# Attention's row maxima: split on VectorE and turned as float16 products a step later; value sums begun by their own products

## The chip, the cores and the metric

The kernel runs on one core of one Trainium2 chip. The metric is device time of one execution in microseconds (us). The core has five engines that each work through a queue of their own in order: TensorE (PE in the profile; PEld is its weight load), VectorE (DVE), ScalarE (ACT), GpSimd (POOL) and SyncE (SP), which issues the DMAs. An instruction waits for semaphores that other engines raise; whatever stands behind it in the same queue waits with it.

## What is computed

One layer over 2048 tokens of width 1024 with a context of 256 tokens: a modulation, a bidirectional retention of 4 heads, grouped attention (8 query heads, 2 key heads, head size 64), an output product, and a feed-forward part of width 4096. The change touches the attention alone:

```python
def _dense_attention(q, k, v):
    s = jnp.einsum('bqkgd,bskd->bkgqs', q, k).astype(jnp.float32) * ATT_SCALE
    p = jax.nn.softmax(s, axis=-1).astype(v.dtype)
    return jnp.einsum('bkgqs,bskd->bqkgd', p, v)
```

Keys and values are those of context and tokens together, 2304 rows, which are 18 tiles of 128.

## The kernel before

The work on 128 tokens is a tile; a `Group` is one tile with one key head and its four query heads. There are 32 groups, `order` counts the tiles from the last to the first and gives each tile an even group (`g` = 0) and an odd one. The program is written out step by step: `on(k, phase, ...)` puts a call into step `k`, and every step runs its calls phase by phase in the order of `PHASES` (scores, piece, maximum, early, exp, cast, low, chain, pe, values, late, dma). A group takes 18 steps for its maxima and, from 22 steps after its first, 18 for its scores, so that in one step TensorE works on the scores of one group and on the maxima of the next. Two groups make a block of 36 steps, into which `retention` and `output_tile` lay their own products (`bank` tiles) and what belongs to them on the other engines.

Per group:

- `piece` and `maximum` (L169 to L187): 18 products of queries and keys into PSUM tiles `mp`, of which there are two, and from each VectorE's negative maxima into `nm`, five for each head and 128 queries.
- `least` (L189 to L193): two reductions of `nm` into columns 64 and 96 of `mt`, a float32 tile with one 128 column part for each head; column 80 holds a constant from the start (L1431).
- `turn` (L195 to L198), a step later: four float32 transposes of `mt` into an `mp` tile, so that the maxima lie along the free axis in rows 64, 80 and 96.
- `rows` (L201): ScalarE writes rows 64 to 127, divided by `ROW` = 8192, as float16 into the second half of the queries `qr`. `rows2` (L205), a step after that: VectorE writes the rest of the division into rows 96 to 127, from the same PSUM tile.
- `scores` (L211, L212): two products into `st`, the second with keys that hold 8192 in rows 64, 80 and 96 (`unit`), which subtracts the maximum. `exp` (L217) makes `p` on ScalarE, two tiles of it are cast to float16 `phi` (`cast`, L221), and the rest becomes `plo` on GpSimd for pairs 0, 2, 4, 6 and 7 (L228) and on VectorE for the others, one half in each of two steps (L230).
- `values` (L232 to L245): products of `plo` (65 columns) and `phi` (129 columns) with the values into the sums `o`. The sums of a group begin with two products of a tile of zeros, 258 columns each (L236).

What stands around it and is named below: `norm` (L1600), two at a time on ScalarE, and the gate product (L1604, `oo<-oo,ogate`) on GpSimd, both of the retention; `add` (L1730, `xr`) on VectorE and `square` (L1737, into `oat`) on ScalarE, of the output tile; L1817 on GpSimd, of `h_pair`, in four of the later blocks; L1670 on VectorE and L1687 on SyncE, once at the beginning, of `output_scales`.

Of the kernel before, what the change touches and what calls it, by code (L numbers as in the profile page):

```python
# [11 lines left out]
F32 = mybir.dt.float32  # L12
F32R = mybir.dt.float32r
F16 = mybir.dt.float16
BF16 = mybir.dt.bfloat16
I32 = mybir.dt.int32
AF = mybir.ActivationFunctionType
ALU = mybir.AluOpType
AX = mybir.AxisListType
# [3 lines left out]
P = 128  # L23
# [6 lines left out]
NK = NT + NC  # L30
H = 4
CH = 128
HD = 64
# [3 lines left out]
PSHIFT = 8  # L37

ROW = 8192.0
VW = 2 * HD + 1  # L40
# [16 lines left out]
def layer_kernel(ctx: ExitStack, tc: tile.TileContext, a: dict, out: bass.AP):  # L57
    nc = tc.nc
    mm = nc.tensor.matmul
# [4 lines left out]
    ident = const.tile([P, P], F32, name="ident")  # L64
# [76 lines left out]
    wv = None  # L141
    early = kp.tile([P, NK * (VW + 1)], F32, name="early", tag="wv")
# [6 lines left out]
    class Group:  # L149
# [14 lines left out]
                nc.sync.dma_start(q[64:, 0, :, e], src[:, 0])  # L164

        def minima(self, pool):
            self.nm = pool.tile([P, 2, 2, 5], F32, name="nm", tag="nm")

        def piece(self, i, pool=None, tag="mp"):  # L169
            m = self.m[i] = (pool or psS).tile([P, 512], F32, name="mp", tag=tag)  # L170
# [17 lines left out]

        def least(self, mt):  # L189
            self.mt = mt  # L190
            nm = self.nm.rearrange("p a b c -> p (a b) c")
            for c in (64, 96):
                nc.vector.tensor_reduce(mt[:, :, c], nm, axis=AX.X, op=ALU.min)  # L193

        def turn(self):  # L195
            self.m = psS.tile([P, 4, P], F32, name="mp", tag="mp")
            for h in range(4):
                nc.tensor.transpose(self.m[:, h], self.mt[:, h], ident)  # L198

        def rows(self):  # L200
            nc.scalar.activation(self.qr[64:, 1], self.m[64:], AF.Copy, scale=1 / ROW)  # L201

        def rows2(self):
            lo = self.qr[96:, 1]
            nc.vector.scalar_tensor_tensor(lo, self.m[96:], 1 / ROW, lo, op0=ALU.mult, op1=ALU.subtract)  # L205

        def scores(self, kt):
            ps = self.s[kt] = psS.tile([P, 512], F32, name="st", tag="st")
# [23 lines left out]
        def values(self, j):  # L232
            if j == 0:
                self.o = [psV.tile([P, 2, VW], F32, name=f"o{b}", tag=f"o{b}") for b in range(2)]
                for o in self.o:
                    mm(o, zeros, wv[:, 0, :2, :VW], start=True, stop=False)  # L236
            hi, lo = self.hi.pop(j), self.lo.pop(j)
            for i in range(2):
                v = wv[:, self.g, 2 * j + i]
                for h in range(4):  # L240
                    o = self.o[h // 2][:, h % 2]
                    c = slice(h * P, (h + 1) * P)
                    last = 2 * j + i == NK - 1 and h % 2 == 1
                    mm(o[:, : HD + 1], lo[:, i, c], v[:, : HD + 1], start=False, stop=False)  # L244
                    mm(o, hi[:, i, c], v[:, :VW], start=False, stop=last)  # L245

        def evacuate(self):
            self.so = op.tile([P, 4, VW], F32, name="so", tag="so")
# [20 lines left out]
    with ExitStack() as st, tc.manual_schedule():  # L269
# [5 lines left out]
        op = st.enter_context(tc.tile_pool(name="op", bufs=2, reuse_waits="tile"))  # L275
# [143 lines left out]
        def turn_rows(end):  # L419
            def use(s, x):  # L420
                def turn():
                    x["t"] = columns(x["b"][:64], 4, psO.tile([P, 4, P], F32, name="psc", tag="pso"))

                do(s, "turn", turn)
                do(s + 1, "vec", lambda: end(x["t"]))

            return use
# [251 lines left out]
        def post(s, g, col, kind, i, x):  # L679
# [23 lines left out]
            if col in (C_RQ, C_RK):  # L703
# [27 lines left out]

                late = s + 4 + (s < 5)
                do(late, "turn", turn)
                do(late + 1, "turned", turned)
                do(late + 2, "store", lambda: nc.sync.dma_start(dst.rearrange("p (h t) -> p h t", h=H), x["z"]))
# [17 lines left out]
            elif col == C_AQ:  # L753
# [12 lines left out]
                    lambda: bc(x["r"].unsqueeze(2), [P, 8, HD]),  # L766
                )
                do(s + 4, "turn", turn)

                def high():  # L770
# [158 lines left out]
        def ff_scales(s):  # L929
# [73 lines left out]
            for i, what in enumerate((bounds, rows, results)):  # L1003
                do(s + 5 + i, "aux", what)
# [181 lines left out]
        units, first = [], {}  # L1186
# [10 lines left out]
        for (g, col), w in weights.items():  # L1197
# [4 lines left out]
            for j in range(w.n):  # L1202
                f, h = s - 5 + j, s - 3 + j if j < 2 else s - 1
                if (g, col) == (1, C_RQ):
                    f, h = s - 9 + j, (s - 6, s - 5, s - 2, s - 2)[j]
                f, h = f - early_by, h - early_by
# [13 lines left out]
        for n, tile_of in enumerate(GROUPS[1]):  # L1220
            b = first[0, C_RV] + 3 + n + n // 6
            rows, x = Rows([tile_of], 1), {}

            def turn(n=n, rows=rows, x=x):
                kind, i = GROUPS[1][n]
                hs[1, n] = new_h(1, kind, i)
                x["p"] = [Part(kind, rows.x[0], hs[1, n], k, 4) for k in (0, 4)]
                for p in x["p"]:
                    p.turn()

            def each(what, x=x):
                for p in x["p"]:
                    getattr(p, what)()

            do(b - 4, "load", rows.load, 0)
            do(b - 2, "hi", rows.square, 0)
            do(b - 1, "hi", rows.root)
            do(b, "vec", rows.norm, 0)
            do(b, "turn", turn)
            do(b + 1, "vec", each, "scale")  # L1240
            do(b + 1, "pool", each, "shift")
            do(b + 2, "hi", each, "high")
            do(b + 3, "low", each, "low")
# [161 lines left out]
    def pool(stack, name, bufs=1, **kw):  # L1405
        return stack.enter_context(tc.tile_pool(name=name, bufs=bufs, reuse_waits="tile", **kw))

    qp = pool(attn, "qp", 2)
    op = pool(attn, "op2", 2)
    vp = pool(attn, "vp")  # L1410
# [11 lines left out]
    for g in range(2):  # L1422
        nc.sync.dma_start(ks2[:64, g], ks[:64, g])
        nc.sync.dma_start(ks2[64:, g], a["unit"])
    zeros = vp.tile([P, P], F16, name="zeros")
    nc.vector.memset(zeros, 0.0)
    mts = [vp.tile([P, 4, P], F32, name=f"mt{i}") for i in range(2)]
    for mt in mts:
        nc.gpsimd.memset(mt, 0.0)

        nc.gpsimd.memset(mt[:, :, 80], PSHIFT * math.log(2.0) * HD**0.5)  # L1431

    def bank(i, shape=(P, 4, P)):
        return psX.tile(list(shape), F32, name=f"bank{i}", tag=f"bank{i}")
# [3 lines left out]
    def on(k, phase, fn, *args):  # L1438
        events.setdefault((k, phase), []).append((fn, args))
# [28 lines left out]
    def attention():  # L1468
        for n, g in enumerate(groups):
            k = NK * n  # L1470
            if n > 0:
                if n > 1:
                    on(k - 14, "dma", g.load)
                on(k - 1, "late", g.minima, sm)
                for i in range(NK):
                    on(k + i, "piece", g.piece, i)
                    on(k + i + 1, "maximum", g.maximum, i)
            on(k + NK, "chain", g.least, mts[n % 2])
            on(k + NK + 1, "piece", g.turn)
            on(k + NK + 2, "cast", g.rows)  # L1480
            on(k + NK + 3, "early", g.rows2)
            k += LAG
            for i in range(NK):
                on(k + i, "scores", g.scores, i)
                on(k + i + 1, "exp", g.exp, i)
            for j in range(NK // 2):
                on(k + 2 * j + 3, "cast", g.cast, j)
                if j in POOL_PAIRS:
                    on(k + 2 * j + 4, "low", g.low, j)
                else:  # L1490
                    for i in range(2):
                        on(k + 2 * j + 4 + i, "low", g.low, j, i)
                on(k + 2 * j + 7, "values", g.values, j)
            k += NK + 6
            on(k, "cast", g.evacuate)
            on(k + 1, "chain", g.invert)
            on(k + 1, "late", g.combine, ats)
        return NK * len(groups) + LAG + 9
# [307 lines left out]
    def h_pair(hf, j, k):  # L1806
# [28 lines left out]
        for at, i, w in forms:  # L1835
            on(k + at, "late", form, i, w)
            on(k + at + 3, "dma", store, i)

    done = attention()
    retention(26)  # L1840
    output_weights(24)
# [451 lines left out]
    with tc.manual_schedule():  # L2293
# [8 lines left out]
        k = min(events)[0]  # L2302
# [69 lines left out]
```

## Time and profile before

| what | value |
|---|---|
| median of 3 runs | 2705.83 us (2702.64 to 2707.8) |
| profiled execution: its time | 2705.45 us |
| profiled execution: its span | 2703.5 us |
| mean granted TensorE clock | 0.990 |
| first and last turn of a group (L198) | 617.4 and 1483.5 us |
| busy in the span | PE 97%, DVE 75%, ACT 56%, POOL 64% |

The span goes from the first to the last instruction; the time of the execution is 1.95 us longer. A row of the timeline gives the start in us, the duration, the engine, the line, the operation, output and inputs, their shape and a count; what stands in brackets at its end is how long the engine had been idle and which instruction ended that. A row of the waits gives who waited for whom, the total in us, how often, and the longest. Products on TensorE overlap: their pace is read from start to start. Attention lies between about 617 and 1510 us; what comes before is the projections, what comes after the feed-forward part.

### The profile page before, as it was taken

To read this page: it belongs to the slowest core of one execution; us is meant where nothing else is said; L and a number is where in the kernel's file an instruction comes from. 1 tells how busy PE (TensorE), PEld (TensorE's weight loads), DVE (VectorE), ACT (ScalarE), POOL (GpSimd) and SP (SyncE) were. 2 spreads that over 40 slices of the span, in tenths; PEclk is the share of its full clock that TensorE was granted. 3 is DMA by queue.
4 is the path that set the end of the run, shared out by engine and by line. 5 is a ranking of instruction groups with operands and counts; after the bars stand their busy time and mean duration, and the time that the engine had idled before them with its cause. 6 is when DMAs were issued, how large, how long until landed. Compare 5 with 4: busy or idle time off the path is not lost.

```text
span 2703.5 us, 45665 instructions
## 1 busy us (share of the span) xinstructions
PE 2626.2 (97%) x16756; PEld 1473.1 (54%) x16756; DVE 2028.8 (75%) x3030; ACT 1527.0 (56%) x2572; POOL 1728.2 (64%) x1349
## 2 busy tenths in 40 slices
PE   6999999997999999999999999999999999999998
PEld 3876555545666666666666544444444444444443
DVE  3688798666888888888888497889877566556586
ACT  2655443424887778878888576666666322222243
POOL 2545466634666667787877596777654467666686
PEclk8999999998999999999999999999999999999999
DMA  6766999746122212323232565666694847574453
GB/s 230 250 230 187 310 324 339 261 124 182 42 78 67 68 54 86 118 76 90 80 111 67 209 200 150 216 217 224 220 324 133 291 163 281 179 293 161 170 179 118
DMA packets 325353, 480.09 MB, mean 178 GB/s; under 512 B 82308, under 2 KB 192516, under 8 KB 320648
## 3 DMA queue, kind: packets, MB, share of 16 engines
q1 hardware_dynamic: 324744, 476.90, 53.6%
q8 instruction: 132, 2.16, 0.3%
q14 instruction: 93, 0.76, 0.1%
q10 hardware_dynamic: 384, 0.26, 0.0%
HBM read 320.10 MB, written 156.38 MB: 176 GB/s over the span
## 4 chain that ended last, share of the span: by engine, by line
PE 84%; DVE 6%; DMA 4%; ACT 3%; issue 2%; POOL 0%; SPq 0%; ACTq 0%; DVEq 0%; POOLq 0%
PE pd L2183 7%; PE pd L2185 7%; PE pd L2184 7%; PE pu L1958 7%; PE pu L1956 7%; PE pu L1957 7%; PE pso L1184 4%; PE pso L1182 4%; PE pso L1183 4%; PE o L245 4%; PE st L211 4%; PE st L212 4%; PE mp L174 3%; PE o L244 2%; PE bank L1725 2%; PE bank L1723 2%
## 5 line engine op out<-in xcount | busy, mean ns | idle before, releaser
L187 DVE TENSOR_REDUCE nm<-mp 128x1 f32<-128x512 f32 (+1 forms) x576 | 391.8, 686 | 142.4 <-PE mp L174 124.9
L228 POOL TENSOR_TENSOR plo<-p,phi 128x1024 f16<-128x1024 f32 x160 | 345.6, 2161 | 154.6 <-ACT phi L221 133.3
L217 ACT ACTIVATE p<-st 128x512 f32<-128x512 f32 x576 | 340.6, 597 | 155.3 <-PE st L212 145.4
L1956 PE MATMUL pu<-hf,w1f 128*128 128x512 f16 x896 | 339.6, 379 | 0.0
L1957 PE MATMUL pu<-hf,w1f 128*128 128x512 f16 x896 | 339.6, 379 | 0.0
L1958 PE MATMUL pu<-hf,w1f 128*128 128x512 f16 x896 | 339.6, 379 | 0.0
L2183 PE MATMUL pd<-w,uf 128*128 128x512 f16 x896 | 339.6, 379 | 0.0
L2184 PE MATMUL pd<-w,uf 128*128 128x512 f16 x896 | 339.6, 379 | 0.0
L2185 PE MATMUL pd<-w,uf 128*128 128x512 f16 x896 | 339.6, 379 | 0.0
L2203 POOL TENSOR_TENSOR y<-y,d 128x512 f32<-128x512 f32 x128 | 210.4, 1646 | 147.2 <-ACT uf L2172 99.8
L221 ACT ACTIVATE phi<-p 128x1024 f16<-128x1024 f32 x288 | 303.9, 1055 | 0.0
L230 DVE TENSOR_TENSOR plo<-p,phi 128x512 f16<-128x512 f32 x256 | 234.2, 916 | 20.1 <-ACT phi L221 7.8
L245 PE MATMUL o<-wv,phi 128*128 128x129 f16 x2304 | 240.2, 220 | 0.0
L211 PE MATMUL st<-qr,ks 128*128 128x512 f16 x576 | 220.1, 382 | 14.9 <-ACT p L217 14.8
L244 PE MATMUL o<-wv,plo 128*128 128x65 f16 x2304 | 232.5, 193 | 0.0
L212 PE MATMUL st<-qr,ks 128*128 128x512 f16 x576 | 219.9, 382 | 0.0
L244 PEld LDWEIGHTS <-plo 128*128 128x128 f16 x2304 | 207.8, 98 | 22.0 <-issue 0.6
L245 PEld LDWEIGHTS <-phi 128*128 128x128 f16 x2304 | 204.8, 97 | 23.4
L2195 DVE SCALAR_TENSOR_TENSOR y<-pd,scy,y 128x512 f32<-128x512 f32 x160 | 116.8, 747 | 131.9 <-PE pd L2185 131.7
L1968 DVE TENSOR_TENSOR r<-pu,r 128x512 f32<-128x512 f32 x224 | 149.9, 684 | 83.5 <-PE pu L1958 59.6
L1182 PE MATMUL pso<-wf,h_l 128*128 128x512 f16 (+1 forms) x576 | 208.2, 361 | 0.0
L1184 PE MATMUL pso<-wf,h_l 128*128 128x512 f16 (+1 forms) x576 | 208.1, 361 | 0.0
(364 smaller groups left out, 6119.5 us busy)
## 6 DMA issues: line engine op xcount, KB each, us to landing
wm<-in_w_ff SPq DMA_DIRECT2D x64, 512.0 KB, 7.6
u<-r SPq DMA_DIRECT2D x128, 256.0 KB, 4.3
ur<-u SPq DMA_DIRECT2D x128, 256.0 KB, 5.8
y<-x SPq DMA_DIRECT2D x64, 512.0 KB, 6.9
wf<-w2f SPq DMA_DIRECT2D x112, 256.0 KB, 2.9
w<-wf SPq DMA_DIRECT2D x28, 1024.0 KB, 8.9
w1r<-in_w_ff SPq DMA_DIRECT2D x48, 512.0 KB, 5.3
x<-y SPq DMA_DIRECT2D x48, 512.0 KB, 2.9
```

The costliest lines, as they stand in the source:

```text
L187: nc.vector.tensor_reduce(dst, src, axis=AX.X, op=ALU.max, negate=True)
L211: mm(ps, ks[:, self.g, k], q[:, 0], start=True, stop=False)
L217: nc.scalar.activation(self.p[kt // 2][:, kt % 2], self.s.pop(kt), AF.Exp, scale=HD**-0.5)
L228: nc.gpsimd.tensor_tensor(lo, p, hi, op=ALU.subtract)
L244: mm(o[:, : HD + 1], lo[:, i, c], v[:, : HD + 1], start=False, stop=False)
L245: mm(o, hi[:, i, c], v[:, :VW], start=False, stop=last)
L1956: mm(pu[hf, i], whi, hi, start=k == 0, stop=False)
L1957: mm(pu[hf, i], whi, lo, start=False, stop=False)
L1958: mm(pu[hf, i], wlo, hi, start=False, stop=k == 3)
L2183: mm(ps, u[:, 0, b], w[:, b, 0], start=b == 0, stop=False)
L2184: mm(ps, u[:, 0, b], w[:, b, 1], start=False, stop=False)
L2185: mm(ps, u[:, 1, b], w[:, b, 0], start=False, stop=b == 3)
```

## The change

`least` now reduces `nm` once into a sixth column, and writes its 8192nd part as float16 into column 64 of `mt` and the rest of that division into column 96. `mt` is float16 and has a fifth part, a copy of the identity. `turn` is four ordinary float16 products of a part of `mt` with that identity, and stands a step later, in the step of `rows`. `rows` only copies, and `rows2` is gone. In `values` the first product of a group is that of `phi`, whose start flag begins the sums; the tile of zeros and its two products are gone.

```diff
-            nm = self.nm.rearrange("p a b c -> p (a b) c")
-            for c in (64, 96):
-                nc.vector.tensor_reduce(mt[:, :, c], nm, axis=AX.X, op=ALU.min)
+            m = self.nm.rearrange("p a b c -> p (a b) c")
+            nc.vector.tensor_reduce(m[:, :, 5], m[:, :, :5], axis=AX.X, op=ALU.min)
+            nc.vector.tensor_scalar_mul(mt[:, :4, 64], m[:, :, 5], 1 / ROW)
+            nc.vector.scalar_tensor_tensor(
+                mt[:, :4, 96], m[:, :, 5], 1 / ROW, mt[:, :4, 64], op0=ALU.mult, op1=ALU.subtract
+            )
...
-                nc.tensor.transpose(self.m[:, h], self.mt[:, h], ident)
+                mm(self.m[:, h], self.mt[:, h], self.mt[:, 4], start=True, stop=True)
...
-            nc.scalar.activation(self.qr[64:, 1], self.m[64:], AF.Copy, scale=1 / ROW)
-
-        def rows2(self):
-            lo = self.qr[96:, 1]
-            nc.vector.scalar_tensor_tensor(lo, self.m[96:], 1 / ROW, lo, op0=ALU.mult, op1=ALU.subtract)
+            nc.scalar.activation(self.qr[64:, 1], self.m[64:], AF.Copy)
...
-                for o in self.o:
-                    mm(o, zeros, wv[:, 0, :2, :VW], start=True, stop=False)
...
-                    last = 2 * j + i == NK - 1 and h % 2 == 1
+                    first, last = j == i == 0, 2 * j + i == NK - 1 and h % 2 == 1
+                    if first:
+                        mm(o, hi[:, i, c], v[:, :VW], start=h % 2 == 0, stop=False)
                     mm(o[:, : HD + 1], lo[:, i, c], v[:, : HD + 1], start=False, stop=False)
-                    mm(o, hi[:, i, c], v[:, :VW], start=False, stop=last)
+                    if not first:
+                        mm(o, hi[:, i, c], v[:, :VW], start=False, stop=last)
...
-    zeros = vp.tile([P, P], F16, name="zeros")
-    nc.vector.memset(zeros, 0.0)
-    mts = [vp.tile([P, 4, P], F32, name=f"mt{i}") for i in range(2)]
+    mts = [vp.tile([P, 5, P], F16, name=f"mt{i}") for i in range(2)]
...
+        nc.gpsimd.tensor_copy(mt[:, 4], ident)
...
-            on(k + NK + 1, "piece", g.turn)
+            on(k + NK + 2, "piece", g.turn)
             on(k + NK + 2, "cast", g.rows)
-            on(k + NK + 3, "early", g.rows2)
```

Lines behind L188 of the changed kernel are one or two lower than before (`scores` L210 and L211, `exp` L216, `cast` L220, `low` L227 and L229, `rows` L204, `turn` L201).

How it stands in the queues, at the turn of the even group that the prediction follows (the 15th of the 32). TensorE before: the turn is behind the scores of its step, and behind it come the step's piece and the values.

```order
L211 LDWEIGHTS ks
L211 MATMUL st<-qr,ks 128x512
L212 LDWEIGHTS ks_6650
L212 MATMUL st<-qr,ks_6650 128x512
L198 MATMUL mp<-ident,mt_6657 128x128 x4
L174 LDWEIGHTS qr
L174 MATMUL mp<-ks,qr 128x512
L244 LDWEIGHTS plo
L244 MATMUL o_12446<-wv,plo 128x65
```

TensorE now, a step later in the program; what is left out are the further three products of the turn.

```order
L211 LDWEIGHTS ks_6650
L211 MATMUL st<-qr,ks_6650 128x512
L201 LDWEIGHTS mt_6655
L201 MATMUL mp<-mt_6655 128x128
...
L174 LDWEIGHTS qr
L174 MATMUL mp<-ks,qr 128x512
L1721 LDWEIGHTS ah
L1721 MATMUL bank_12496<-wo,ah 128x512
```

The values have moved ahead of the turn, and behind it now stand that step's piece and three products of the output tile.

ScalarE at the same place, as the changed program has it (before, its order is the same):

```order
L216 ACTIVATE p_12612<-st 128x512
L204 ACTIVATE qr<-mp 64x512
L1598 ACTIVATE oo<-oo,mr,cy_gn 128x128 x2
L216 ACTIVATE p_12659<-st 128x512
L220 ACTIVATE phi<-p_12612 128x1024
L216 ACTIVATE p_12659<-st 128x512
L1598 ACTIVATE oo<-oo,mr,cy_gn 128x128 x2
```

`rows` (the copy into `qr`) keeps its place ahead of the two norms and the next exponential, while the turn that it needs comes a step later on TensorE.

VectorE before, from `least` to the sum `xr`, and then now:

```order
L193 TENSOR_REDUCE mt_6657<-nm 128x4 x2
L187 TENSOR_REDUCE nm<-mp 128x1
L230 TENSOR_TENSOR plo<-p_12536,phi 128x512
L187 TENSOR_REDUCE nm<-mp 128x1 x2
L205 SCALAR_TENSOR_TENSOR qr<-mp,qr 32x512
L187 TENSOR_REDUCE nm<-mp 128x1 x3
L230 TENSOR_TENSOR plo<-p_12687,phi 128x512
```
```order
L192 TENSOR_REDUCE nm<-nm 128x4
L193 TENSOR_SCALAR mt_6655<-nm 128x4
L194 SCALAR_TENSOR_TENSOR mt_6655<-nm,mt_6655 128x4
L187 TENSOR_REDUCE nm<-mp 128x1
L229 TENSOR_TENSOR plo<-p_12508,phi 128x512
L187 TENSOR_REDUCE nm<-mp 128x1 x5
L229 TENSOR_TENSOR plo<-p_12659,phi 128x512
```

Two small operations have become three, and `rows2` (L205 before) is gone from among the maxima.

More of the change, by code (lines that the diff above doesn't have):

```diff
@@ L166, in minima @@
         def minima(self, pool):
-            self.nm = pool.tile([P, 2, 2, 5], F32, name="nm", tag="nm")
+            self.nm = pool.tile([P, 2, 2, 6], F32, name="nm", tag="nm")
         def piece(self, i, pool=None, tag="mp"):
@@ L1424, in layer_kernel @@
         nc.sync.dma_start(ks2[64:, g], a["unit"])
-    zeros = vp.tile([P, P], F16, name="zeros")
-    nc.vector.memset(zeros, 0.0)
-    mts = [vp.tile([P, 4, P], F32, name=f"mt{i}") for i in range(2)]
+    mts = [vp.tile([P, 5, P], F16, name=f"mt{i}") for i in range(2)]
     for mt in mts:
         nc.gpsimd.memset(mt, 0.0)
-        nc.gpsimd.memset(mt[:, :, 80], PSHIFT * math.log(2.0) * HD**0.5)
+        nc.gpsimd.memset(mt[:, :4, 80], PSHIFT * math.log(2.0) * HD**0.5 / ROW)
+        nc.gpsimd.tensor_copy(mt[:, 4], ident)
     def bank(i, shape=(P, 4, P)):
```

## Prediction

> **What bounds the kernel now.** I read the page's engine table first, then a window in the middle of attention, then TensorE's own waits from 650 to 1510 us, then the timeline of one block of 36 steps. The first row is the page's, the second the window's (busy time by engine, granted clock, DMA share), the third the waits'.
>
> ```profile
> PE 2626.2 (97%) x16756; PEld 1473.1 (54%) x16756; DVE 2028.8 (75%) x3030; ACT 1527.0 (56%) x2572; POOL 1728.2 (64%) x1349
> ```
> ```profile
> 950.00:1050.00 100.00, 98.37 (x936) 64.47 (x933) 83.19 (x146) 78.96 (x131) 64.34 (x50) 1.00 0.24 78
> ```
> ```profile
> PE st L211 <- ACT p L217: 14.8, 33, 0.6
> ```
>
> TensorE is busy 98.4% in the attention stage, at full granted clock, and waits there for ScalarE for only 14.8 us in 33 places. But ScalarE is at 79% and VectorE at 83%, and both work in order: whoever is held up inside a block may have no slack there. So the change is priced twice, on TensorE alone, and then through the queues.
>
> **TensorE's share.** From the timeline: the two products with zeros, then the first values' products (a 65 and a 129 column one in turn), then a turn (four transposes) and the piece behind it.
>
> ```profile
> 1001.19 0.39 PE L236 MATMUL o<-wv,zeros 128*128 128x258 f16 x2
> 1001.41 0.19 PE L244 MATMUL o<-wv,plo 128*128 128x65 f16 x1
> 1001.45 0.22 PE L245 MATMUL o<-wv,phi 128*128 128x129 f16 x1
> 1001.50 0.19 PE L244 MATMUL o<-wv,plo 128*128 128x65 f16 x1
> ...
> 1013.10 0.60 PE L198 MATMUL mp<-ident,mt 128*128 128x128 f32 x4
> 1013.53 0.38 PE L174 MATMUL mp<-ks,qr 128*128 128x512 f16 x1
> ```
>
> Read starts, not durations, since products overlap. The zeros take 1001.41 - 1001.19 = 0.22 us a group, and go. The turn takes 1013.53 - 1013.10 = 0.43, and goes. Four float16 products of 128 columns come. The trace has none of that size; a pair of 65 and 129 columns takes 0.09, so one of 128 takes over half of it and less than all: four take 0.18 to 0.36. By columns (0.09 x 128 / 194) it is 0.06 each, 0.23 for four; I take that, as the 129 column row is nearest. TensorE saves 0.22 + 0.43 - 0.23 = 0.42 a group; 32 groups give 13.4 us if nothing else moves.
>
> The Trainium skill, "TensorE: Matmul & The Clock Gate", Part 4, puts one 128x128 transpose at about 275 ns within a kernel. By that, as an estimate, the four removed ones would be 1.1 us and the saving 1.1 a group, 35 us in all; but the rows above show four in 0.43, so the measurement decides, and this rule gets no chance below.
>
> **The step later, in a block with even group.** Two groups make a block of 36 steps (about 55 us) with one output tile. Here is ScalarE at the even group's turn (the turn of 1013.10), with pauses ahead of an instruction in brackets; what is left out between runs back to back.
>
> ```profile
> 1013.44 0.59 ACT L217 ACTIVATE p<-st 128x512 f32<-128x512 f32 x1
> 1014.06 0.59 ACT L201 ACTIVATE qr<-mp 64x512 f16<-64x512 f32 x1
> 1014.67 0.88 ACT L1600 ACTIVATE oo<-oo,mr,cy_gn 128x128 f32<-128x128 f32 x2
> 1015.58 0.60 ACT L217 ACTIVATE p<-st 128x512 f32<-128x512 f32 x1
> ...
> 1017.02 0.59 ACT L217 ACTIVATE p<-st 128x512 f32<-128x512 f32 x1
> ...
> 1018.74 1.05 ACT L221 ACTIVATE phi<-p 128x1024 f16<-128x1024 f32 x1
> 1019.69 0.60 ACT L217 ACTIVATE p<-st 128x512 f32<-128x512 f32 x1
> 1021.07 0.60 ACT L217 ACTIVATE p<-st 128x512 f32<-128x512 f32 x1 [0.79 <-PE st L212]
> ```
> ```profile
> 1014.45 0.38 PE L211 MATMUL st<-qr,ks 128*128 128x512 f16 x1
> ...
> 1017.09 0.38 PE L211 MATMUL st<-qr,ks 128*128 128x512 f16 x1
> ...
> 1018.38 0.38 PE L211 MATMUL st<-qr,ks 128*128 128x512 f16 x1
> ```
>
> `rows` (L201) keeps its place in ScalarE's queue: behind one exponential, ahead of two norms and the next exponential. Before, its turn lay a step earlier and was long done. Now the turn stands behind the scores of the same step. Those start at 1014.45 - 0.43 = 1014.02 and take 0.43 (two products at the piece's pace); the turn issues from 1014.45 to 1014.68, and its last result is there at 1014.62 + 0.22 = 1014.84. `rows` then starts at about 1014.87 instead of 1014.06: ScalarE pauses and all behind it comes 0.81 later, until the pause of 0.79 at 1021.07 swallows it.
>
> That pause is too late to help three waiters. First TensorE: the scores of 1017.09 need the exponential of 1015.58, now 1016.39 to 1016.99; TensorE, 0.20 ahead, would be there at 1016.89 and starts at 1017.05. The next scores, 1.29 behind (as 1018.38 - 1017.09), would start at 1018.34; they need the exponential of 1017.02, now over at 1018.42, and start at about 1018.49: another 0.15 of waiting. TensorE is then 0.11 later than before, and the turn's 0.20 is lost. The other waiters are GpSimd and VectorE (POOL and DVE):
>
> ```profile
> 1017.20 2.13 POOL L228 TENSOR_TENSOR plo<-p,phi 128x1024 f16<-128x1024 f32 x1 [1.44 <-ACT phi L221]
> 1019.28 1.27 POOL L1604 TENSOR_TENSOR oo<-oo,ogate 128x512 f32<-128x512 f32 x1
> ...
> 1022.69 2.13 POOL L228 TENSOR_TENSOR plo<-p,phi 128x1024 f16<-128x1024 f32 x1 [2.14 <-ACT phi L221]
> ```
> ```profile
> 1019.95 1.15 DVE L230 TENSOR_TENSOR plo<-p,phi 128x512 f16<-128x512 f32 x1
> 1021.23 0.69 DVE L187 TENSOR_REDUCE nm<-mp 128x1 f32<-128x512 f32 x1
> 1021.83 0.68 DVE L230 TENSOR_TENSOR plo<-p,phi 128x512 f16<-128x512 f32 x1
> ...
> 1023.03 0.74 DVE L1730 SCALAR_TENSOR_TENSOR xr<-bank,sco,xr 128x512 f32<-128x512 f32 x1
> ```
> ```profile
> 1023.81 0.63 ACT L1737 ACTIVATE oat<-xr 128x512 f32<-128x512 f32 x1 [0.71 <-DVE xr L1730]
> ```
> ```profile
> 1026.50 0.38 PE L211 MATMUL st<-qr,ks 128*128 128x512 f16 x1 [0.24 <-ACT p L217]
> ...
> 1029.45 0.38 PE L211 MATMUL st<-qr,ks 128*128 128x512 f16 x1 [0.58 <-ACT p L217]
> ```
>
> The `plo` at 1019.95 takes 1.15 where that of 1021.83 takes 0.68: it ends 0.55 after GpSimd's gate product (1019.28 + 1.27 = 1020.55), so it stood until that was over. Its `phi` of 1018.74 will end at 1020.60. GpSimd's `plo` moves from 1017.20 to 1018.01, so its gate product runs from 1020.09 to 1021.36, and VectorE's `plo` ends 0.55 later, at 1021.91. The maximum of 1021.23 starts at 1021.83, 0.60 later, and so do the sum `xr` at 1023.03, the square behind it on ScalarE, and the two exponentials for which TensorE already waits 0.24 and 0.58. **Such a block gets 0.60 longer**, and the zeros saved within it (between those two waits) only lengthen a wait. Ends of this term: 0.42 shorter, if no lateness arrives, and the second rival's price.
>
> In four later blocks GpSimd has a further product there:
>
> ```profile
> 1074.94 1.73 POOL L1604 TENSOR_TENSOR oo<-oo,ogate 128x512 f32<-128x512 f32 x1
> ...
> 1076.63 1.27 POOL L1817 TENSOR_TENSOR hb<-hb 128x512 f32<-128x512 f32 x1
> ```
> ```profile
> 1074.85 0.69 DVE L230 TENSOR_TENSOR plo<-p,phi 128x512 f16<-128x512 f32 x1
> ...
> 1076.73 1.72 DVE L230 TENSOR_TENSOR plo<-p,phi 128x512 f16<-128x512 f32 x1
> ```
>
> There VectorE is already held until the end of that product (1077.90). With the first `plo` (1074.85) 0.7 later, the gate product goes ahead undisturbed to 1076.21, that `plo` behind it to 1076.76, the further product then until 1078.0, 0.10 later than before, and VectorE's second `plo` behind that. So these blocks get 0.10 longer.
>
> **Odd groups.** ScalarE behind their `rows`:
>
> ```profile
> 1040.93 0.59 ACT L201 ACTIVATE qr<-mp 64x512 f16<-64x512 f32 x1
> 1042.66 0.60 ACT L217 ACTIVATE p<-st 128x512 f32<-128x512 f32 x1 [1.14 <-PE st L212]
> ```
>
> A pause of 1.14 follows and no norms, so a later `rows` moves the next exponential by only some 0.3, and TensorE does not come to wait for it. The full 0.42 is kept.
>
> **Edits at nothing.** `least` has three dependent operations on four columns instead of two (0.24 together); by that row I allow 0.3 more. In the even group this is hidden:
>
> ```profile
> 1011.46 0.24 DVE L193 TENSOR_REDUCE mt<-nm 128x4 f32<-128x20 f32 x2
> 1012.22 0.69 DVE L187 TENSOR_REDUCE nm<-mp 128x1 f32<-128x512 f32 x1 [0.52 <-PE mp L174]
> ```
>
> VectorE waits 0.52 for the next score anyway; without that cover the price would be 32 x 0.3 = 9.6. `rows2` leaves VectorE (about a maximum's 0.69) between pieces that it waits for: nothing gained. The turn's PSUM tile now comes free when `rows` ends (1015.46), and the piece queued for it stands at 1015.97; behind that piece stand the values and next scores. The margin is 0.5. Two copies of the identity (128 columns each) run once on GpSimd with the fills ahead of the stage: between nothing and, by its 1.27 for 512 columns, 2.5; I take nothing, since no product of TensorE needs them before the first turn.
>
> **Start.** Before, the first turn held one of two `mp` tiles and the piece behind it waited for VectorE. Now that piece goes first, into the free tile, so VectorE's second maximum and this reduction come some 0.7 sooner, and with it SyncE's transfers, for which the stage's beginning waits:
>
> ```profile
> 622.07 0.16 DVE L1670 TENSOR_REDUCE oat<-wmx 128x1 f32<-128x16 f32 x1
> ```
> ```profile
> 622.26 0.32 SPq L1687 DMA_DIRECT2D ind<-oat  x1
> ```
>
> I take 0.7 gained, between 0 and 0.8.
>
> **Sum.** 16 odd groups: -6.7. Group 0: -0.7. Group 2, before output tiles begin: -0.4. Ten blocks: +6.0. Four: +0.4. Together -1.4 on the profiled execution's 2705.45 (span 2703.5; the median of the runs is 2705.83): **2704.0**.
>
> **Rivals.** (1) *All of TensorE's saving arrives*, because the lateness ends inside ScalarE's pauses: 2705.45 - 13.4 = 2692.0; halfway, with even blocks unchanged, 2698. For it: TensorE at 98.4%. Against it: ScalarE has no pause between 1014.06 and 1020.29. (2) *VectorE comes second at the next collision*, and the kernel is slower. After the shift its second `plo` starts at 1022.43 and GpSimd's of 1022.69 at about 1022.73. Decided by 0.30: were VectorE that much later, it would stand through 2.13, and end at 1022.73 + 2.13 + 0.55 = 1025.41 instead of 1023.11. Such a block then costs 0.60 + 2.30 = 2.9; ten of them 29, in all 2727; three or four of them, some 2712. For it: the margin is thin; against it: both chains hang on the same ScalarE queue and shift together. That fewer products run than the diff says is excluded by the order of the changed program.
>
> **How the numbers follow.** Forecast (2700.5 to 2711) 0.50; rival 1, whole or half, 0.28; rival 2 0.22. A measurement tells about 0.2% (5.4 us) from no change, so these are same, faster and slower. The range runs from rival 1's end, 2691.5, to 2712, where rival 2's first blocks lie; most of rival 2 is left out.
>
> **What would show it.** Right: four turn products within 0.25; `rows` preceded by a pause of 0.8 in even groups; two new waits of the scores for `p` of about 0.15 right behind; the square some 0.6 later; TensorE busy less by about 13 but the span not. Wrong: no pause ahead of `rows`; a `plo` of over 2 us on VectorE in even blocks; pieces waiting for `qr`.

## The result and the profile after

The changed kernel takes 2721.73 us (median of four runs, 2716.75 to 2725.61) against 2706.82 us before (four runs, 2702.64 to 2709.39): a ratio of 1.0051, 95% interval 1.0028 to 1.0073. It is some 14.9 us slower, where 1.8 less were forecast. The profiled execution took 2720.09 us, with a span of 2718.3.

The engine table of the changed kernel:

```profile
PE 2619.4 (96%) x16692; PEld 1458.0 (54%) x16692; DVE 2034.2 (75%) x3029; ACT 1527.6 (56%) x2572; POOL 1736.1 (64%) x1351
```

TensorE is busy 2626.2 - 2619.4 = 6.8 us less, in a span that is 14.8 longer: it waits. Where, its own waits from 650 to 1530 us tell (who waited for whom, total, times, longest):

```profile
PE st L210 <- ACT p L216: 20.5, 35, 0.6
PE mp L174 <- DVE nm L187: 11.2, 6, 2.2
```

The wait of the scores for ScalarE is the row of before, grown from 14.8 to 20.5. The second row is nearly new: a product of the maxima waits for VectorE, four times for over 2 us. Two windows of 100 us show how unevenly this lies (busy time of each engine, then the granted clock, the DMA share and GB/s):

```profile
950.00:1050.00 100.00, 97.47 (x914) 62.75 (x912) 79.66 (x145) 78.25 (x130) 65.00 (x50) 1.00 0.23 73
1050.00:1150.00 100.00, 94.85 (x898) 62.51 (x897) 83.39 (x142) 79.65 (x133) 77.35 (x60) 0.98 0.31 88
```

To place it, I measure a block of 36 steps from the turn of one even group to that of the next. Between the turns of groups 4 and 30 lie thirteen blocks. Nine of them are *plain*; in the other four, the prediction's "four later blocks", GpSimd also has the work of `h_pair`. Before, a plain block took 54.90 to 54.94 us and one of the four 55.93 or 55.94. Now a plain one takes 55.04 to 55.11, and the four take 59.68, 57.76, 57.75 and 59.65. The nine add 1.4 us, the four add 3.75 + 1.82 + 1.81 + 3.71 = 11.1, and 2.1 lie ahead of group 4 and behind group 30: 14.6 together, the difference of the two profiled executions.

This is the odd group of the first of the four, before; of the timeline, VectorE's and GpSimd's rows around `least`:

```profile
1094.13 1.71 POOL L1556 TENSOR_TENSOR oqf<-oqt,tf 128x512 f32<-128x512 f32 x1
...
1094.64 0.24 DVE L193 TENSOR_REDUCE mt<-nm 128x4 f32<-128x20 f32 x2
...
1095.03 0.69 DVE L187 TENSOR_REDUCE nm<-mp 128x1 f32<-128x512 f32 x1
...
1095.64 0.76 DVE L230 TENSOR_TENSOR plo<-p,phi 128x512 f16<-128x512 f32 x1
...
1095.81 1.72 POOL L1556 TENSOR_TENSOR oqb<-oqt,tb 128x512 f32<-128x512 f32 x1
...
1097.49 2.13 POOL L228 TENSOR_TENSOR plo<-p,phi 128x1024 f16<-128x1024 f32 x1
```

And the same place in the changed kernel (L192 to L194 are `least`, L201 the turn, L174 a product of the maxima):

```profile
1097.16 1.73 POOL L1554 TENSOR_TENSOR oqf<-oqt,tf 128x512 f32<-128x512 f32 x1
...
1097.68 0.16 DVE L192 TENSOR_REDUCE nm<-nm 128x4 f32<-128x20 f32 x1
...
1097.87 1.05 DVE L193 TENSOR_SCALAR mt<-nm 128x4 f16<-128x4 f32 x1
...
1098.85 1.27 POOL L1554 TENSOR_TENSOR oqb<-oqt,tb 128x512 f32<-128x512 f32 x1
...
1098.95 1.20 DVE L194 SCALAR_TENSOR_TENSOR mt<-nm,mt 128x4 f16<-128x4 f32 x1
...
1100.06 0.68 DVE L187 TENSOR_REDUCE nm<-mp 128x1 f32<-128x512 f32 x1
1100.08 2.12 POOL L227 TENSOR_TENSOR plo<-p,phi 128x1024 f16<-128x1024 f32 x1
...
1100.66 2.08 DVE L229 TENSOR_TENSOR plo<-p,phi 128x512 f16<-128x512 f32 x1
1100.79 0.38 PE L201 MATMUL mp<-mt 128*128 128x128 f16 x4
...
1102.67 0.68 DVE L187 TENSOR_REDUCE nm<-mp 128x1 f32<-128x512 f32 x1
...
1103.40 0.50 PE L174 MATMUL mp<-ks,qr 128*128 128x512 f16 x1 [2.23 <-DVE nm L187]
```

Read it downward. Two operations on four columns take 1.05 and 1.20 us, and each ends with a product of GpSimd: 1097.87 + 1.05 = 1098.92 against 1097.16 + 1.73 = 1098.89, and 1100.15 against 1100.12. The two reductions of before ran through in 0.24 while the same product went on. So the next maximum (L187) starts 2.38 us behind `least`'s first row, GpSimd goes straight into its `plo`, and VectorE's own `plo`, a moment behind, stands until that is over: 2.08 us in place of 0.76. The maximum behind it frees one of the two `mp` tiles only at 1103.35. The next product is due in that one, since the turn took the other, and TensorE pauses 2.23 us.

In a plain block GpSimd reaches the same two products earlier, since no work of `h_pair` lies ahead of them; there the second ends at 1041.93, and the changed `least` costs next to nothing:

```profile
1042.40 0.16 DVE L192 TENSOR_REDUCE nm<-nm 128x4 f32<-128x20 f32 x1
...
1042.60 0.18 DVE L193 TENSOR_SCALAR mt<-nm 128x4 f16<-128x4 f32 x1
...
1042.81 0.18 DVE L194 SCALAR_TENSOR_TENSOR mt<-nm,mt 128x4 f16<-128x4 f32 x1
```

The Trainium skill, "SBUF — State Buffer", "Who interferes with whom", states a rule that fits: VectorE and GpSimd share one pair of SBUF ports as an exclusive lock, held for the whole instruction. A VectorE operation needs it when it has two inputs in SBUF, or one input and a mode that uses both ports (`tensor_scalar` is named); a `tensor_reduce` never does on this chip. The rows agree: L193, L194 and `plo` stand, the reductions don't.

Two of the four pauses cost more than themselves. Two windows of TensorE's clock around the pause of 2.23 us, and TensorE's timeline behind the second of the four pauses, of 2.07:

```profile
1101.00:1104.00 3.00, 0.77 (x6) 0.30 (x3) 3.00 (x4) 2.13 (x3) 1.75 (x2) 0.92 0.00 0
1104.00:1107.00 3.00, 3.00 (x8) 1.03 (x7) 1.13 (x2) 0.60 (x1) 2.56 (x2) 0.51 0.01 3
```
```profile
1217.89 0.38 PE L174 MATMUL mp<-ks,qr 128*128 128x512 f16 x1 [2.07 <-DVE nm L187]
1218.11 0.38 PE L1721 MATMUL bank<-wo,ah 128*128 128x512 f16 x1
```

Behind 2.23 us the granted clock is 0.51 for a window of 3 us; behind 2.07 us the products come at their full pace of 0.22 at once. So goes the fourth like the first and the third like the second: two blocks lose 3.7 and two 1.8. The difference of 1.9 is the pause, longer by 0.16, and half of the 3.41 us at half clock, 1.71. Why two pauses lower the clock and two don't, the last section works out from the trace.

### The profile page after: what moved, and what is told of

The parts are those of the page before. It is cut to its first block, busy times and chain, and to the rows that moved or that the text cites. A ratio compares the mean times of both kernels' runs of the same rounds, so it can differ in the third digit from the quotient of the medians.

```text
span 2718.3 us, 45481 instructions
## 1 busy us (share of the span) xinstructions
PE 2619.4 (96%) x16692; PEld 1458.0 (54%) x16692; DVE 2034.2 (75%) x3029; ACT 1527.6 (56%) x2572; POOL 1736.1 (64%) x1351
## 4 chain that ended last, share of the span: by engine, by line
PE 79%; DVE 9%; ACT 6%; issue 3%; DMA 2%; POOL 0%; SPq 0%; DVEq 0%; ACTq 0%; POOLq 0%
PE pd L2181 7%; PE pd L2183 7%; PE pd L2182 7%; PE pu L1956 7%; PE pu L1955 7%; PE pu L1954 7%; PE pso L1184 4%; PE pso L1182 4%; PE pso L1183 4%; PE st L210 3%; PE o L245 3%; PE st L211 3%; PE mp L174 3%; ACT phi L220 2%; ACT p L216 2%
## 5 line engine op out<-in xcount | busy, mean ns | idle before, releaser
L187 DVE TENSOR_REDUCE nm<-mp 128x1 f32<-128x512 f32 (+1 forms) x576 | 391.8, 685 | 143.6 <-PE mp L174 127.3
L227 POOL TENSOR_TENSOR plo<-p,phi 128x1024 f16<-128x1024 f32 x160 | 351.8, 2199 | 151.7 <-ACT phi L220 132.0
L216 ACT ACTIVATE p<-st 128x512 f32<-128x512 f32 x576 | 341.2, 597 | 132.5 <-PE st L211 129.0
L220 ACT ACTIVATE phi<-p 128x1024 f16<-128x1024 f32 x288 | 303.9, 1055 | 0.0
L229 DVE TENSOR_TENSOR plo<-p,phi 128x512 f16<-128x512 f32 x256 | 239.4, 937 | 29.0 <-ACT phi L220 18.2
L210 PE MATMUL st<-qr,ks 128*128 128x512 f16 x576 | 220.0, 382 | 20.7 <-ACT p L216 20.5
L245 PE MATMUL o<-wv,phi 128*128 128x129 f16 x2176 | 229.5, 220 | 0.0
L211 PE MATMUL st<-qr,ks 128*128 128x512 f16 x576 | 220.2, 382 | 0.0
L174 PE MATMUL mp<-ks,qr 128*128 128x512 f16 x512 | 196.5, 384 | 17.0 <-DVE nm L187 15.1
```

Of the source, the lines that this page charges most:

```text
L187: nc.vector.tensor_reduce(dst, src, axis=AX.X, op=ALU.max, negate=True)
L216: nc.scalar.activation(self.p[kt // 2][:, kt % 2], self.s.pop(kt), AF.Exp, scale=HD**-0.5)
L220: nc.scalar.activation(hi, self.p[j], AF.Copy)
L227: nc.gpsimd.tensor_tensor(lo, p, hi, op=ALU.subtract)
```

## Experiments

Theory A: the loss is those two small operations of `least`, which stand behind GpSimd, and what follows from it. Theory B: it is the turn a step later, with `rows` behind it. Theory C: the values' new order. Each ratio is to the kernel before on the same chip. Block lengths are those of the profiled execution. The first plain block still takes up what the start left (it takes 55.1 to 55.6 in all but the kernel before), so plain blocks stand here from the second on, and the first with the two blocks ahead of it in the last column.

| kernel | ratio | 95% interval | plain blocks, us | the four, us | first three blocks, us |
|---|---|---|---|---|---|
| before | 1 | | 54.90 to 54.93 | 55.93, 55.94 | 176.1 |
| changed | 1.0051 | 1.0028 to 1.0073 | 55.04 to 55.11 | 57.75 to 59.68 | 177.2 |
| values only | 0.9987 | 0.9978 to 0.9995 | 54.68 to 54.79 | 55.72, 55.73 | 179.7 |
| `least` of reductions | 1.0006 | 0.9997 to 1.0015 | 55.05 to 55.29 | 55.53 to 55.55 | 176.5 |
| GpSimd's work moved | 1.0008 | 0.9999 to 1.0017 | 55.05 to 55.09 | 55.57 to 55.58 | 177.9 |
| pair added to before | 1.0046 | 1.0033 to 1.0059 | 54.97 to 55.07 | 57.91 to 58.18 | 182.3 |
| one small operation | 1.0008 | 0.9999 to 1.0017 | 55.05 to 55.31 | 55.75 to 55.93 | 176.1 |
| turn sooner | 1.0018 | 1.0009 to 1.0026 | 54.54 to 54.94 | 57.10 to 57.11 | 181.4 |
| reductions, turn sooner | 0.9969 | 0.9957 to 0.9981 | 54.45 to 54.69 | 54.63, 54.64 | 178.6 |
| reductions, `rows` later | 0.9973 | 0.9962 to 0.9983 | 54.25 to 54.73 | 55.49 to 55.51 | 175.7 |

**Values only.** The kernel before, with the part in `values` alone:

```diff
-                for o in self.o:
-                    mm(o, zeros, wv[:, 0, :2, :VW], start=True, stop=False)
...
+                    first, last = j == i == 0, 2 * j + i == NK - 1 and h % 2 == 1
+                    if first:
+                        mm(o, hi[:, i, c], v[:, :VW], start=h % 2 == 0, stop=False)
...
```

> The kernel before with the third part of the change alone: no products with zeros, the sums begun by the values' own products; minima, turn, rows and rows2 as before. Theory A (the loss comes from the small operations of least on VectorE, which stand behind GpSimd's products in the odd groups of four blocks): this part has no share in the loss and saves TensorE 0.22 us a group, so 2706.8 - 32 x 0.22 = 2699.8 us, or as little as 2703 where an even group's wait for ScalarE swallows it. Theory C (the loss comes from the values' new order): 2712 or above.

Measured: 2703.79 us against 2706.47. Theory C falls: this part saves. The blocks of the table are 0.15 to 0.22 us shorter, which is about one group's 0.22 and not two, so one of a block's two groups loses its saving again. The whole is a little under what either end of the expectation gave (2.7 of 3.5 to 7); in the profiled run the first three blocks took 3.7 longer. The trace shows a collision there that the edit doesn't touch: three small operations of `output_scales` on VectorE stand beside GpSimd (L1678, L1679 and L1681 take 1.00, 2.05 and 0.89 us, at most 0.16 each before). How much of the 3.7 this makes is not settled.

**`least` of reductions alone.** The changed kernel, with the contested operations replaced by a form that should not stand:

```diff
-            nc.vector.tensor_reduce(m[:, :, 5], m[:, :, :5], axis=AX.X, op=ALU.min)
-            nc.vector.tensor_scalar_mul(mt[:, :4, 64], m[:, :, 5], 1 / ROW)
-            nc.vector.scalar_tensor_tensor(
-                mt[:, :4, 96], m[:, :, 5], 1 / ROW, mt[:, :4, 64], op0=ALU.mult, op1=ALU.subtract
-            )
+            nc.vector.tensor_reduce(mt[:, :4, 64], m[:, :, :5], axis=AX.X, op=ALU.min)
+            nc.vector.tensor_reduce(m[:, :, 5], m[:, :, :5], axis=AX.X, op=ALU.min)
+            nc.vector.tensor_reduce(m[:, :, 6], mt[:, :4, 64:65], axis=AX.X, op=ALU.min, negate=True)
+            with nc.allow_low_precision(reason="the low part"):
+                nc.vector.tensor_reduce(mt[:, :4, 96], m[:, :, 5:7], axis=AX.X, op=ALU.add)
...
```

What is left out: `nm` gets a seventh column, and the division by `ROW` goes back into `rows`.

> The changed kernel with least made of four reductions in place of one reduction, a TENSOR_SCALAR and a SCALAR_TENSOR_TENSOR (one more small operation than the change has; the factor 1/ROW goes back into rows); all else as changed. Theory A: what stands behind GpSimd is the form of the operation, and reductions don't (before, two of them took 0.24 at the same place while GpSimd's product ran), so the four odd groups lose their 1.8 to 3.8 us each, and the time goes to 2721.7 - 11 = 2710.7, or to 2708 if the start gets its 1.5 to 3 back too. Theory B (the turn a step later, with the copy into qr behind it, costs the time): 2720 to 2723, as before the edit.

Measured: 2707.93 us. The first of the four odd groups, in the timeline of this run:

```profile
1096.89 1.73 POOL L1554 TENSOR_TENSOR oqf<-oqt,tf 128x512 f32<-128x512 f32 x1
...
1097.41 0.17 DVE L192 TENSOR_REDUCE mt<-nm 128x4 f16<-128x20 f32 x1
1097.49 0.16 DVE L193 TENSOR_REDUCE nm<-nm 128x4 f32<-128x20 f32 x1
...
1097.61 0.16 DVE L194 TENSOR_REDUCE nm<-mt 128x4 f32<-128x4 f16 x1
1097.80 0.17 DVE L196 TENSOR_REDUCE mt<-nm 128x4 f16<-128x8 f32 x1
...
1097.88 0.68 DVE L187 TENSOR_REDUCE nm<-mp 128x1 f32<-128x512 f32 x1
...
1098.48 0.68 DVE L229 TENSOR_TENSOR plo<-p,phi 128x512 f16<-128x512 f32 x1
1098.57 1.72 POOL L1554 TENSOR_TENSOR oqb<-oqt,tb 128x512 f32<-128x512 f32 x1
```

One operation more, on the same four columns, and the maximum starts 0.47 behind the first reduction in place of 2.38, while GpSimd's product runs. VectorE's `plo` now starts well ahead of GpSimd's and takes 0.68. The four blocks are back below their old length; the plain ones are not. So theory A holds for the 11.1 us, and the plain blocks' growth is left for B.

**The other party moved.** If it is a collision, it must also go when GpSimd is elsewhere. In the changed kernel, two calls of `h_pair` were put six steps later, behind `oqf` and `oqb`:

```diff
-        on(k + 29, "late", add, "t4", "b21", "t2", "t1")
-        forms = [(6, 0, "b11"), (10, 3, "b21"), (14, 6, "b22"), (28, 5, "t1")]
+        on(k + 35, "late", add, "t4", "b21", "t2", "t1")
+        forms = [(6, 0, "b11"), (10, 3, "b21"), (14, 6, "b22"), (34, 5, "t1")]
```

> The changed kernel with two GpSimd steps of the four later blocks (the fourth split and the fourth difference of h_pair) moved six steps later, behind the two products oqf and oqb, so that these end before least begins, as in the other blocks; least and all else as changed. Theory A: least's small operations take 0.18 each there, and the four odd groups lose their 1.8 to 3.8 us, 2710 to 2712, unless the moved products meet VectorE again (then up to 2716). Theory B: 2720 to 2723.

Measured: 2709.65 us. The timeline at the same place:

```profile
1097.14 1.27 POOL L1554 TENSOR_TENSOR oqb<-oqt,tb 128x512 f32<-128x512 f32 x1
...
1098.88 0.16 DVE L192 TENSOR_REDUCE nm<-nm 128x4 f32<-128x20 f32 x1
...
1099.08 0.18 DVE L193 TENSOR_SCALAR mt<-nm 128x4 f16<-128x4 f32 x1
...
1099.29 0.18 DVE L194 SCALAR_TENSOR_TENSOR mt<-nm,mt 128x4 f16<-128x4 f32 x1
```

The very operations that took 1.05 and 1.20 us take 0.18 each once GpSimd's product is over (1098.41), and the four blocks take 55.57. Nothing in `least`, the turn or the values differs from the changed kernel.

**The pair added to the kernel before.** The converse: nothing of the change but the two operations, and nobody waits for what they write.

```diff
             for c in (64, 96):
-                nc.vector.tensor_reduce(mt[:, :, c], nm, axis=AX.X, op=ALU.min)
+                nc.vector.tensor_reduce(mt[:, :, c], nm[:, :, :5], axis=AX.X, op=ALU.min)
+            nc.vector.tensor_scalar_mul(nm[:, :, 5], mt[:, :, 96], 1 / ROW)
+            nc.vector.scalar_tensor_tensor(
+                nm[:, :, 6], mt[:, :, 96], 1 / ROW, nm[:, :, 5], op0=ALU.mult, op1=ALU.subtract
+            )
...
```

> The kernel before, with the change's two small operations (TENSOR_SCALAR, then SCALAR_TENSOR_TENSOR, 128x4) added behind the two reductions of least; they write spare columns of nm that nobody reads, and all else is as before. Theory A: they stand behind oqf and oqb in the four blocks, the maximum behind them comes 2 us late, VectorE's plo falls behind GpSimd's, and each of the four blocks takes 1.2 to 3.8 us more: 2711 to 2722. Rival (what stands or costs is not the operations but the float16 tile or the turn that reads it): 2706.5 plus 32 x 0.3 at the most where VectorE has no slack, blocks of 54.9 and 55.9 to 56.2: 2706 to 2709.

Measured: 2721.19 us against 2708.33. This alone makes the old kernel about as slow as the changed one. Its timeline shows the same chain:

```profile
1101.99 0.96 DVE L194 TENSOR_SCALAR nm<-mt 128x4 f32<-128x4 f32 x1
...
1102.88 1.26 POOL L1560 TENSOR_TENSOR oqb<-oqt,tb 128x512 f32<-128x512 f32 x1
1102.98 1.19 DVE L195 SCALAR_TENSOR_TENSOR nm<-mt,nm 128x4 f32<-128x4 f32 x1
...
1104.11 2.12 POOL L232 TENSOR_TENSOR plo<-p,phi 128x1024 f16<-128x1024 f32 x1
1104.69 2.09 DVE L234 TENSOR_TENSOR plo<-p,phi 128x512 f16<-128x512 f32 x1
```

The rival (the float16 tile or its turn) falls: both are absent here. The four blocks lose 2.0 to 2.2 us each, 8.5 together, and in the profiled run the first three blocks 6.2.

**One small operation in place of two.** The changed kernel, `least` of two reductions and one SCALAR_TENSOR_TENSOR:

```diff
-            nc.vector.tensor_reduce(m[:, :, 5], m[:, :, :5], axis=AX.X, op=ALU.min)
-            nc.vector.tensor_scalar_mul(mt[:, :4, 64], m[:, :, 5], 1 / ROW)
+            nc.vector.tensor_reduce(mt[:, :4, 64], m[:, :, :5], axis=AX.X, op=ALU.min)
+            nc.vector.tensor_reduce(m[:, :, 5], m[:, :, :5], axis=AX.X, op=ALU.min)
             nc.vector.scalar_tensor_tensor(
-                mt[:, :4, 96], m[:, :, 5], 1 / ROW, mt[:, :4, 64], op0=ALU.mult, op1=ALU.subtract
+                mt[:, :4, 96], m[:, :, 5], 1.0, mt[:, :4, 64], op0=ALU.mult, op1=ALU.subtract
             )
...
```

> The changed kernel with least made of two reductions and one SCALAR_TENSOR_TENSOR (1/ROW back in rows): one operation of the contested form in place of two. Theory A: it stands only until the first of GpSimd's two products ends, the maximum starts 1.1 sooner than in the changed kernel, VectorE's plo comes ahead of GpSimd's, and the four blocks lose under 0.5 us each: 2708 to 2711. If what decides is that any such operation stands there at all: 2715 to 2721.

Measured: 2711.67 us (0.7 above the expected end), against 2708.33 for the kernel before on that chip. The timeline there:

```profile
1097.61 1.72 POOL L1554 TENSOR_TENSOR oqf<-oqt,tf 128x512 f32<-128x512 f32 x1
...
1098.40 0.96 DVE L194 SCALAR_TENSOR_TENSOR mt<-nm,mt 128x4 f16<-128x4 f32 x1
...
1099.28 0.68 DVE L187 TENSOR_REDUCE nm<-mp 128x1 f32<-128x512 f32 x1
...
1099.88 1.23 DVE L229 TENSOR_TENSOR plo<-p,phi 128x512 f16<-128x512 f32 x1
...
1100.52 2.58 POOL L227 TENSOR_TENSOR plo<-p,phi 128x1024 f16<-128x1024 f32 x1
```

The operation still stands, for 0.96 us, but VectorE's `plo` now comes ahead of GpSimd's, and these blocks take only 0.2 to 0.4 us more than with reductions. Standing there is cheap as long as the order behind it holds; the second operation is the one too many, because with it the two `plo` change places.

**The turn sooner.** The changed kernel with the turn at its old step, one line: `on(k + NK + 1, "piece", g.turn)`.

> The changed kernel with its turn back at the step it had before, all else as changed. Theory A: VectorE's order is the same, and its two small operations still stand behind GpSimd until 1100, so the four groups still lose 1.8 to 3.8 us; the turn now stands ahead of a piece and so waits for least itself: 2720 to 2728. Theory B (the later turn costs the time): 2702 to 2708.

Measured: 2712.01 us. Neither theory as I had put it gives this: A said 2720 to 2728, B 2702 to 2708. VectorE's chain is the same to 0.01 us, but TensorE's waits in it are now three (timeline):

```profile
1098.34 0.40 PE L201 MATMUL mp<-mt 128*128 128x128 f16 x4 [1.33 <-DVE mt L194]
...
1098.92 0.38 PE L174 MATMUL mp<-ks,qr 128*128 128x512 f16 x1 [0.19 <-DVE nm L187]
...
1101.54 0.38 PE L174 MATMUL mp<-ks,qr 128*128 128x512 f16 x1 [0.46 <-DVE nm L187]
```

They sum to 1.98 us, the longest is 1.33, and the clock stays at 1.00 in the windows of 3 us there. I had the turn's wait come on top of the other; it is part of the same one. The collision still costs 57.1 - 54.63 = 2.5 us a block (against the next run, which differs in `least` alone), where with the later turn it cost 2.2 in two blocks and 4.1 in two. So the later turn had a share in the loss of the four after all: it gathers the wait in one place, long enough for the clock to fall.

**Reductions and the turn sooner.** Both edits together.

> The kernel of the run with four reductions in least, with its turn a step sooner (where it was before the change). Theory A, with what the runs so far showed: the later turn cost 0.26 us a block (55.06 against 54.80), so 16 blocks give 4 us: 2704, with blocks of 54.8 and 55.3. If the later turn is worth nothing once least is quick: 2707 to 2708.

Measured: 2701.08 us against 2708.33, with the next run the fastest here. With a quick `least`, taking the turn back is worth 0.4 to 0.8 us in a plain block and 0.9 in each of the four, more than I expected. Why the four gain more was not traced.

**Reductions and `rows` later.** If the later turn costs by holding up ScalarE, it must also help to leave the turn late and to move `rows` out of its way: `on(k + NK + 3, "cast", g.rows)`.

> The kernel of the run with four reductions in least, with rows a step later, so that ScalarE doesn't pause for the turn. Theory A for the even groups (rows behind the turn holds up ScalarE by some 0.8, and this is the 0.15 by which the undisturbed blocks grew): 54.8 in place of 55.06 to 55.30, 2704. Rival (the tile that the turn holds, freed by rows, costs the time): it is held a step longer, and the blocks grow to 55.1 to 55.7, 2708 to 2717.

Measured: 2701.92 us. ScalarE's `rows` of one even group in the changed kernel and in this run:

```profile
1017.50 0.59 ACT L204 ACTIVATE qr<-mp 64x512 f16<-64x512 f32 x1 [0.83 <-PE mp L201]
```
```profile
1020.93 0.59 ACT L204 ACTIVATE qr<-mp 64x512 f16<-64x512 f32 x1
```

The pause of 0.83 is gone, and plain blocks are 0.4 to 0.9 us shorter than with `rows` right behind the turn. The rival, that the tile held by the turn is what costs, falls: it is held longer here. So theory B is right for the plain blocks. The four (55.50 against 55.53) gain nothing from it.

## Why the prediction was wrong, step by step

- **TensorE's share: right.** The turn takes 0.22 us where 0.23 was worked out, and the zeros' 0.22 shows in the blocks of the run with the values only. The sign named for it, busy time less by about 13, did not come: it fell by 6.8. That sum moves with the clock, since a product of 512 columns lasts 0.63 in the slow stretches in place of 0.38; what else is in it was not traced (in the other kernels with all these products it fell by 7.8 to 12.9).
- **The step later, even group: right in mechanism and in size.** `rows` pauses 0.83 (0.81 forecast). The two further waits came, 0.14 each, too short for the list of waits: the scores start 0.20 behind the last product of the values (1019.45 and 1019.65) where it was 0.06 (1017.03 and 1017.09), and the next scores 0.36 behind the product ahead of them (1020.73 and 1021.09) where it was 0.21 (1018.17 and 1018.38). Measured from the scores of the step ahead (1012.67 before, 1015.30 now), `xr` comes 0.59 later, where 0.60 was forecast: it moved from 1023.03 to 1026.25. A plain block was to become 0.60 - 0.42 = 0.18 longer and became 0.14 to 0.19 longer. With a quick `least` and the turn back, where no lateness is left, it is mostly 0.4 shorter than before and not twice 0.42: from the even turn to the odd one about 0.2, and about 0.2 on to the next even one. So it is not shown that an odd group of a plain block keeps its full 0.42; where the rest goes was not traced.
- **Edits at nothing: this step failed.** It priced the new operations by the 0.24 us of two reductions, a row of another form, and looked for cover only in the even group, where VectorE waits 0.52 anyway. In the odd group of the four blocks the two new ones take 2.25 us in place of 0.36, because GpSimd is in the middle of a product there. The trace had two kinds of rows that told this: `plo` on VectorE standing behind GpSimd's gate product, which the prediction itself read, and the reductions going through beside a product.
- **Odd groups, "the full 0.42 is kept": failed with it.** It was read off ScalarE's pause of 1.14, with no look at VectorE. For the four blocks the terms gave 0.10 - 0.42 = -0.32 each, -1.3 in all; they measured +11.1. That is 12.4 of the 16.1 us between forecast and profiled execution.
- **Start: failed in sign.** The reduction that it named did come 0.77 sooner against the last row of the stage before (`wmx`, L745, at 619.50 and the reduction at 622.07 before; 618.06 and 619.86 now), as forecast, but the gain was lost again. For what lies outside the thirteen blocks the terms gave -1.8; it was +2.1. The trace shows two more collisions there. One is in group 1's `least` (timeline):

```profile
657.97 0.81 DVE L193 TENSOR_SCALAR mt<-nm 128x4 f16<-128x4 f32 x1
...
658.82 1.19 DVE L194 SCALAR_TENSOR_TENSOR mt<-nm,mt 128x4 f16<-128x4 f32 x1
...
661.16 0.38 PE L201 MATMUL mp<-mt 128*128 128x128 f16 x4 [1.89 <-DVE nm L187]
```

The other is in `output_scales`, whose nine small operations on VectorE, one column each, took 1.44 us from first to last before, with GpSimd idle. Now they take 3.92, as two of those with two inputs stand beside GpSimd, and a product of the maxima behind them waits 3.86. This is the last of them:

```profile
640.65 1.97 DVE L1682 TENSOR_TENSOR inv<-inv,oat 128x1 f32<-128x1 f32 x1
```

This second collision is not the change's own: each of the other runs has it too (2.2 to 4.9 us for the nine), the one where only `values` was edited among them. Before, TensorE had its long wait for VectorE later, 4.79 at 655.77. How much of the 2.1 either makes, the runs do not settle: the first three blocks scatter from 175.7 to 182.3 us among the kernels.
- **Rivals.** The second named the right event, VectorE second behind GpSimd's `plo` for over 2 us. It put it into the even groups, where the margin of 0.30 held, and not into the odd groups of the four, where the new operations used up a margin of 1.85 (VectorE's `plo` at 1095.64, GpSimd's at 1097.49). The first did not come, but was no idle bound: with a quick `least` and the turn at its old step, the change's products do make the kernel faster, by 0.3%.

## What to carry to other kernels

Price a small VectorE operation by its form and by what GpSimd does at that moment, not by its width, and look at every place of the loop where it will stand, the odd group and the rare block too. Where it would stand, try a form that doesn't: four reductions for two operations took most of the loss back. And ask which two instructions behind it would change places, since an order that turns around cost more here than the delay that turned it.

## What the runs showed of the hardware

- Operations of four columns on VectorE, a TENSOR_SCALAR from float32 and a SCALAR_TENSOR_TENSOR with two inputs in SBUF, took 0.18 us beside an idle GpSimd and 0.81 to 1.20 beside a product of GpSimd of 512 columns, which they outlasted by a few hundredths. Beside GpSimd's operation of four columns at L1459 (685.84 to 687.32) they took 0.18 all the same (686.55 and 686.77). Reductions of four columns took 0.16 to 0.18 either way, also with float16 input or output.
- After a pause of TensorE of 2.23 us in a busy stream (twice) its granted clock was 0.50 for 3.41 us (1103.51 to 1106.92 and 1444.85 to 1448.26) and 1.00 on both sides; after 2.07 us (twice) it stayed at 1.00. The two slow stretches start 341.34 us apart, which is 100 times 3.413. If the time is cut at that step throughout, either pause of 2.23 lies whole in the step ahead of its slow stretch (TensorE idle for 2.23 and 2.22 of it), while the pauses of 2.07 lie across a cut, and no step holds more than 1.74 and 1.91 us of them. A step on the same grid near the start, 659.78 to 663.19, was idle for 2.06 in several pauses, the longest of 1.89, and a slow one followed it. So it is the idleness within a step that counts, and not the length of a single pause. The Trainium skill, "TensorE: Matmul & The Clock Gate", Part 1, puts the window that decides this at about 3.4 us and calls it free-running. The length of the slow stretches and their fixed step agree with that; these rows show besides that about 2.1 us of idleness in it can be enough.
